# When weights are summed, split and released in a two-layer decoder trunk on one core

## The chip, the core and the metric

One core of one Trainium2 chip. The metric is the device time of one execution in microseconds (us); the kernel before has been run three times, and its median is the time that counts. Traces are of one profiled execution. Engines: PE (TensorE), DVE (VectorE), ACT (ScalarE), POOL (GpSimd) and SP (SyncE, which here only issues DMAs).

## The reference

512 tokens of width 1024 pass through two layers. Each layer is an attention and an MLP, each followed by a scaled residual sum and a layer norm:

```python
for l in range(DEPTH):                       # DEPTH = 2
    if l < n_a: y = _mla(x, ...)             # layer A: latent attention, 8 heads
    else:       y = _swa(x, w_q, sinks, w_o, k_band, v_band, rel_bias)  # layer B
    x = _layernorm(alpha * x + y, ln_mix_g[l], ln_mix_b[l])
    x = _layernorm(alpha * x + _mlp(x, mlp_w_up[l], mlp_w_down[l]), ...)
```

`_mlp` is `h = relu(x @ w_up); (h * h) @ w_down` with an inner width of 4096. `_swa` is attention in a sliding window of 128 tokens: 16 query heads of 64 on 4 key and value heads, a bias per head and distance, and a learned sink in the softmax's denominator. Everything is fp32.

## The kernel before

**Products.** PE multiplies in a shorter format (fp32r), so each operand is split into a high and a low part (`split`): ACT copies the high part (L77), DVE or POOL subtracts it from the original to give the low part (L81), and each product is made of three matmuls (L105). So every weight tile costs a DMA into a raw tile, an ACT copy `wh<-raw` of about 1.06 us, and a subtraction `wl<-raw,wh` before PE can use it.

**The stream of weights.** All weights stand in one list, `stream`, in the order of their use. `weights(name)` takes the next one for PE and, ahead of that, prepares others (`prep`: DMA, copy, subtraction are put into the program there): up to AHEAD = 4 tiles ahead on a ring of four `wh` and four `wl` tiles and two raw tiles, but never past `state["hold"]`. `prepare(n)` raises the hold by n and prepares up to it. Where in the program `prep` is called decides, with priorities and the times that a scheduler assigns, where the copy and the subtraction stand in the queues of ACT, DVE and POOL. Queues are served in order: an instruction that waits holds up all behind it. `behind(x)` adds an order after x; `pin` fixes a place.

**The MLP** multiplies in seven products instead of eight (as in Strassen's scheme); some of their weights are sums of two tiles. `grown` (L190 to L201) splits the tile as it is and then lets a DMA from POOL's queue add the next tile to it in place (L200, `accum_op=ALU.add`). The first weights of an MLP are made aside of the ring (`aside`) while the attention's output is still being projected. Two of them are grown: their accumulate DMAs are issued at 165.8 us in layer A and at 648.7 us in layer B.

**Layer norm** of a block t of 128 tokens (`layer_norm`, L428 to L443): DVE aggregates mean and variance (L434), POOL raises the variance to -1/2 (`rsqrt_of`, L413: the inverse deviation `rs`), DVE subtracts the mean and multiplies by the gain (L437), then multiplies by `rs` and adds the offset (L440). In the MLP's input the block is then turned by PE (`XFactors.turn`, L678: eight transposes into two banks) and copied by ACT and DVE (L682, L683, L689). Blocks go 0 to 3; POOL's queue holds the accumulate DMAs ahead of `rs` of block 0.

**The start of layer B** (`begin`, L589 to L618): keys of the first tokens, then two turnings of token blocks (`turn_tokens`, L452, split at L361 and L81) with values between them. The value weights `w_v` are released by `state["hold"] = len(stream)` at L598.

**Attention of layer B** (545 to 631 us) runs through `run_steps` (L533): for each head u it issues the scores of head u+2, some filling work (`fill`: queries of later heads, two heads to a weight tile of `w_sq`, and from head 11 on the output projection), the turning of head u and the mix of head u-1. Per head:
- PE makes scores; DVE adds the bias and takes the maximum (L1332, L1336); ACT takes exponentials (L1340) and the sink's (L1344, into `ri`); DVE adds and inverts (L1345, L1346); POOL multiplies (L1347, L1349).
- `turn`: PE transposes the probabilities into two banks, four transposes for the first half (128x512) and three for the second (128x384), L1360 and L1362. ACT copies each half (`pth`, L77) and DVE subtracts (`ptl`, L81). The first half's copy is ordered behind the latest exponential in the program. A later turning can use the bank when `ptl` is done.
- `mix`: PE multiplies by the values; ACT copies a half (`low`, L1391), DVE adds (L1392). After an odd head ACT copies `oh` (L77) and POOL subtracts `ol`.
- `queries`: eight groups of three matmuls; ACT and DVE put the two heads' queries aside (L1303, L1304). The bias tile comes by a DMA (L1283).

The weights inside this loop are prepared by `weights("w_sq")`, at the start of each tile's use.

Of the kernel before, what the change touches and what calls it, by code (L numbers as in the profile page):

```python
# [11 lines left out]
ALU = mybir.AluOpType  # L12
# [13 lines left out]
SQH, SKVH, SHD = 16, 4, 64  # L26
# [15 lines left out]
AHEAD_S, AHEAD_B = 3, 2  # L42
# [6 lines left out]
def build(tc, nc, io, out):  # L49
    with ExitStack() as top:  # L50
# [11 lines left out]
        def nm(s):  # L62
            n_names[0] += 1
            return f"{s}_{n_names[0]}"
# [21 lines left out]
        def pe(ins):  # L86
            tc.keep_in_program_order(ins)
# [3 lines left out]
        def behind(pair):  # L91

            both = ExitStack()
            for ins in pair or ():
                both.enter_context(tc.issue_after(ins.ins))
            return both

        def pin(ins):

            if pinned[0]:  # L100
                pe(ins)
# [8 lines left out]
            return [(sh, mh), (sh, ml), (sl, mh)]  # L110


        stream, off_ring = [], []

        fetchers, at_hand, fetched = {}, {}, set()

        def tiles_of_weights(aside=None):

            if aside:
                return aside()  # L120
            wh = wp.tile([P, 1024], F32R, tag="wh", bufs=4, name=nm("wh"))
            wl = wp.tile([P, 1024], F32R, tag="wl", bufs=4, name=nm("wl"))
            return wh, wl

        def raw_tile():
            return wp.tile([P, 1024], F32, tag="raw", bufs=2, name=nm("raw"))
# [40 lines left out]
        def queue_seven(name, key, chunk):  # L167

            quads = {}

            def half(a, jp):
                if a not in quads:
                    if (key, a) == ("U", "a"):
                        quads[a] = xp.tile([P, 4, 512], F32, tag="xt", bufs=8, name=nm("wq"))
                    elif (key, a) == ("U", "b"):
                        quads[a] = gp.tile([P, 4, 512], F32, tag="gb", bufs=1, name=nm("wq"))
                    else:
                        quads[a] = mlp_pool[0].tile([P, 4, 512], F32, tag="quad" + a, bufs=1, name=nm("wq"))  # L180
                return quads[a][:, 2 * jp : 2 * jp + 2, :]

            def flat(ap):
                return ap.rearrange("p a b -> p (a b)")

            def grown(a, jp, *more, aside=None):
                wh, wl = tiles_of_weights(aside)
                after = None
                if aside:
                    after = state.pop("plain", None)  # L190
                elif (key, a, jp, bool(more)) == ("U", "b", 0, True):
                    after = state.get("s4")
                elif (key, a, more) == ("U", "a", (1, 0)):
                    after = state.pop(("s2", jp), None)
                with behind(after):
                    state["last"] = split(
                        wh, wl, flat(half(a, jp)), keep=(a, bool(more)) == ("b", True) and key == "U"
                    )
                if more:
                    nc.gpsimd.dma_start(half(a, jp), chunk(*more, jp), accum_op=ALU.add)  # L200
                return wh, wl  # L201

            def loaded(a, jp, at, *more, aside=None):
                pe(nc.sync.dma_start(half(a, jp), chunk(*at, jp)))
                return grown(a, jp, *more, aside=aside)

            def alone(jp, aside=None):
                raw = raw_tile()
                pe(nc.sync.dma_start(raw.rearrange("p (a b) -> p a b", a=2), chunk(1, 0, jp)))
                wh, wl = tiles_of_weights(aside)  # L210
                with behind(state.pop("f1", None) if key == "D" else None):
                    split(wh, wl, raw)
                return wh, wl

            of = {
                1: lambda jp, aside=None: loaded("a", jp, (0, 0), 0, 1, aside=aside),
                5: lambda jp: grown("a", jp, 1, 1),
                6: lambda jp: grown("a", jp, 1, 0),
                4: lambda jp: grown("a", jp),
                2: alone,  # L220
                3: lambda jp: loaded("b", jp, (1, 1), 0, 1),
                7: lambda jp: grown("b", jp),
            }

            def add(n, asides=(None, None)):
                for jp, aside in enumerate(asides):
                    make = (lambda jp=jp, aside=aside: of[n](jp, aside)) if aside else (lambda jp=jp: of[n](jp))
                    stream.append((name, make))
                    off_ring.append(aside is not None)

            return add
# [52 lines left out]
        first_v = len(stream)  # L284
# [9 lines left out]
        state = {"next": 0, "at": 0, "hold": 0}  # L294
# [6 lines left out]
        def prepare(n):  # L301

            state["hold"] += n
            while state["next"] < state["hold"]:
                prep(state["next"])
                state["next"] += 1
# [20 lines left out]
        class Feat:  # L327
# [11 lines left out]
            def turn(self, t):  # L339
                turn_tokens(t, self)  # L340
# [65 lines left out]
        half = cp.tile([P, 1], F32, name="half")  # L406
# [3 lines left out]

        def rsqrt_of(v):
            r = sp.tile([P, 1], F32, tag="rs", bufs=8, name=nm("rs"))
            nc.gpsimd.tensor_tensor(r, v, half, ALU.pow)  # L413
            return r


# [13 lines left out]
        def layer_norm(t, gb, dst):  # L430

            x = xs[t]
            mv = sp.tile([P, 2], F32, tag="mv", bufs=4, name=nm("mv"))
            pin(nc.vector.bn_aggr(mv, stats[t]))  # L434
            stats[t] = None
            r = rsqrt_of(mv[:, 1:2])
            pin(nc.vector.scalar_tensor_tensor(x, x, mv[:, 0:1], gb[0], ALU.subtract, ALU.mult))  # L437
            cuts = (0, 512, 768, D) if dst is None and t == NT - 1 else (0, D)
            for c in map(slice, cuts, cuts[1:]):
                state["norm"] = nc.vector.scalar_tensor_tensor(x[:, c], x[:, c], r, gb[1][:, c], ALU.mult, ALU.add)  # L440
                pin(state["norm"])
                if dst is None:
                    nc.sync.dma_start(out[t * P : (t + 1) * P, c], x[:, c])  # L443
# [86 lines left out]
                    for t in range(NT):  # L530
                        self.evac(t, slice(512, D), bs[t])

        def run_steps(units, ahead, scores, turn, mix, fill, per, lag, rest):  # L533

            total = sum(f[0] for f in fill)
            n, spent, at = len(units), 0.0, 0
            for u in range(-ahead, n):
                if u + ahead < n:  # L540
                    scores(*units[u + ahead])
                target = total * (u + ahead + 1) / (n + ahead)
                while at < len(fill) and (spent < target or fill[at][1] <= u) and fill[at][2] <= u:
                    fill[at][3]()
                    spent += fill[at][0]
                    at += 1
                if u < 0:
                    continue
                turn(*units[u])
                if u >= lag and (u - lag) % per == per - 1:  # L550
                    mix(units[u - lag][0])
            for f in fill[at:]:
                f[3]()
            for f in rest:
                f()
            for u in range(n, n + lag):
                if (u - lag) % per == per - 1:
                    mix(units[u - lag][0])
# [35 lines left out]
        def begin(src, names, evacs, between):  # L594

            state["hold"] = len(stream)  # L598
            ws = [weights(name) for name in names]

            def products(half_):
                late = []
                for w, evac in zip(ws, evacs):
                    cols = slice(half_ * 256, half_ * 256 + 256)
                    b = bank(256)
                    feat_major(src, w, b, cols)
                    late.append((evac, cols, b))
                return late

            late = products(0)  # L610
            for i, f in enumerate(between):
                with tc.high_priority():
                    src.turn(NT - 2 + i)
                late += f()

            with behind(src.last):
                for evac, *at in late:
                    evac(*at)  # L618
            for evac, *at in products(1):
                evac(*at)  # L620
# [276 lines left out]
        with tc.tile_pool(name="mla", bufs=1) as mp:  # L897
# [301 lines left out]
            fill = []  # L1199
# [32 lines left out]
        with tc.tile_pool(name="swa", bufs=1) as mp:  # L1232
# [164 lines left out]
            fill = []  # L1397
# [12 lines left out]
            for m in range(2):  # L1410
                for part in range(2):
                    queries(m, part)
            run_steps([(h, 0) for h in range(SQH)], AHEAD_B, scores, turn, mix, fill, 1, 1, [])

        gb = lambda: load_gb("mix", 1)
        with tc.tile_pool(name="mlp1", bufs=1) as mp:
# [114 lines left out]
```

## Time and profile before

| what | value |
|---|---|
| median of three runs | 996.81 us (996.02 to 997.32) |
| profiled execution | 997.58 us |
| its span in the trace | 995.8 us |
| PE busy | 983.9 us |
| DVE, ACT, POOL busy | 772.3, 555.2, 215.4 us |
| DMA moved | 149.55 MB, 150 GB/s on average |

PE is busy nearly throughout, so what counts is where PE waits, for whom, and how long. In a row of the timeline the columns are the start in us from the start of the span, the duration, the engine, the line of the kernel, the operation, the output and inputs by name, the shapes, how often, and in brackets the engine's idle time before it and what ended that. In the view of waits the columns are the sum in us, the number of waits and the longest one. Times of PE's successive matmuls overlap in the records, since they are pipelined; gaps of PE are best read from start to start.

### The profile page before, as it was taken

Reading aid. Unit: us, or ns where it says so; the run is one execution under the profiler, and the core shown is the slowest. Engines: PE = TensorE matmul, PEld = TensorE weight load, DVE = VectorE, ACT = ScalarE, POOL = GpSimd, SP = SyncE. Lnnn points to the kernel's source line nnn. Section 1 sums busy time; section 2 is a strip of 40 time slices with the busy share of each in tenths; the row PEclk is TensorE's granted clock in tenths of the full one; section 3 lists DMA queues with packets and bytes.
Section 4 is the critical chain, followed back from the end, with each engine's and each line's share of the span. In section 5 each row is a group of like instructions: output and inputs, shape, how many; then the busy total and the mean of one; then the engine's idle time right before and its main releaser. Section 6 shows DMA issues by size and latency. Waiting matters only on the chain.

```text
span 995.8 us, 15827 instructions
## 1 busy us (share of the span) xinstructions
PE 983.9 (99%) x6103; PEld 887.2 (89%) x6103; DVE 772.3 (78%) x1242; ACT 555.2 (56%) x850; POOL 215.4 (22%) x203
## 2 busy tenths in 40 slices
PE   9999999999999999999999999999999999999997
PEld 9888887998999999998898998889998999999986
DVE  6589858999768769786686778698985886898756
ACT  5556644467547547646145798546763663664620
POOL 1231001121212212210002775112131122023000
PEclk9999999999999999999999999999999999999999
DMA  7421228389789978964132212359698698798422
GB/s 261 144 88 44 70 99 241 93 180 235 141 181 241 170 170 218 225 108 148 64 106 96 85 65 75 105 149 211 179 204 186 165 217 173 166 264 143 119 90 85
DMA packets 60679, 149.55 MB, mean 150 GB/s; under 512 B 5260, under 2 KB 10301, under 8 KB 60605
## 3 DMA queue, kind: packets, MB, share of 16 engines
q0 software_dynamic: 24320, 58.73, 33.0%
q1 hardware_dynamic: 36140, 89.56, 26.7%
q8 instruction: 48, 0.79, 0.3%
q10 hardware_dynamic: 144, 0.26, 0.1%
q14 instruction: 27, 0.21, 0.1%
HBM read 146.41 MB, written 4.22 MB: 151 GB/s over the span
## 4 chain that ended last, share of the span: by engine, by line
PE 93%; DVE 2%; DMA 2%; issue 1%; ACT 1%; POOL 0%; DVEq 0%; SPq 0%; POOLq 0%; ACTq 0%
PE mm L105 85%; PE tr L105 5%; PE tr L1171 1%; DMA wq<-in_up 1%; PE tr L678 1%; PE tr L1360 1%; DMA raw<-in_w_v 1%; ACT wh L77 1%; DVE wl L81 0%; PE tr L1362 0%; DVE x L440 0%; DMA xraw<-in_xT 0%; DVE mm L1332 0%; DVE x L437 0%; POOL wq L200 0%
## 5 line engine op out<-in xcount | busy, mean ns | idle before, releaser
L105 PE MATMUL mm<-wh,fac 128*128 128x512 f32 (+1 forms) x944 | 292.6, 386 | 0.0
L77 ACT ACTIVATE wh<-wq 128x1024 fp32r<-128x1024 f32 x164 | 173.7, 1060 | 183.7 <-PE mm L105 128.3
L81 DVE TENSOR_TENSOR wl<-wq,wh 128x1024 fp32r<-128x1024 f32 x164 | 199.6, 1221 | 70.3 <-ACT wh L77 69.4
L105 PE MATMUL mm<-xth,wh 128*128 128x256 f32 (+1 forms) x928 | 243.4, 290 | 0.0
L105 PE MATMUL mm<-xth,wl 128*128 128x256 f32 (+1 forms) x800 | 233.2, 292 | 0.0
L105 PEld LDWEIGHTS mm<-wh,fac 128*128 128x128 f32 x944 | 176.2, 188 | 35.4 <-DVE fac L81 0.6
L105 PE MATMUL mm<-xtl,wh 128*128 128x256 f32 (+1 forms) x672 | 197.1, 293 | 0.0
L105 PE MATMUL mm<-wl,fac 128*128 128x512 f32 (+1 forms) x472 | 182.3, 386 | 0.0
L105 PEld LDWEIGHTS mm<-xth,wh 128*128 128x128 f32 x928 | 168.6, 192 | 3.1
L105 PEld LDWEIGHTS mm<-xth,wl 128*128 128x128 f32 x800 | 153.2, 192 | 2.6
L77 ACT ACTIVATE wh<-raw 128x1024 fp32r<-128x1024 f32 (+3 forms) x86 | 85.1, 990 | 97.6 <-PE mm L105 57.3
L200 POOL DMA_DIRECT2D wq<-in_up x64 | 77.5, 1228 | 259.4 <-DVE wl L81 191.9
L105 PEld LDWEIGHTS mm<-xtl,wh 128*128 128x128 f32 x672 | 128.7, 192 | 3.0
L81 DVE TENSOR_TENSOR wl<-raw,wh 128x1024 fp32r<-128x1024 f32 (+2 forms) x66 | 77.1, 1174 | 36.1 <-ACT wh L77 35.8
L105 PEld LDWEIGHTS mm<-wl,fac 128*128 128x128 f32 x472 | 88.8, 188 | 16.7
L200 POOL DMA_DIRECT2D wq<-in_down x48 | 42.0, 875 | 187.3 <-DVE wl L81 181.4
L81 POOL TENSOR_TENSOR wl<-raw,wh 128x1024 fp32r<-128x1024 f32 (+2 forms) x20 | 41.2, 2062 | 88.1 <-ACT wh L77 82.1
L105 PE MATMUL mm<-wh,oh 128*128 128x512 f32 x128 | 50.9, 397 | 0.0
L105 PE MATMUL mm<-wh,ol 128*128 128x512 f32 x128 | 50.1, 391 | 0.0
L105 PE MATMUL mm<-wl,oh 128*128 128x512 f32 x128 | 50.0, 391 | 0.0
L413 POOL TENSOR_TENSOR rs<-mv,half 128x1 f32<-128x1 f32 x16 | 9.9, 620 | 168.0 <-DVE mv L434 167.9
L578 DVE TENSOR_TENSOR x<-mm,x 128x512 f32<-128x512 f32 (+1 forms) x49 | 32.9, 675 | 15.8 <-PE mm L105 15.7
(222 smaller groups left out, 1816.0 us busy)
## 6 DMA issues: line engine op xcount, KB each, us to landing
wq<-in_up POOLq DMA_DIRECT2D x64, 512.0 KB, 8.6
wq<-in_down POOLq DMA_DIRECT2D x48, 512.0 KB, 6.9
wq<-in_up SPq DMA_DIRECT2D x32, 512.0 KB, 6.6
raw<-in_down SPq DMA_DIRECT2D x28, 512.0 KB, 6.6
wq<-in_down SPq DMA_DIRECT2D x24, 512.0 KB, 5.0
raw<-in_up SPq DMA_DIRECT2D x16, 512.0 KB, 4.2
raw<-in_w_o SPq DMA_DIRECT2D x8, 512.0 KB, 5.1
raw<-in_w_sq SPq DMA_DIRECT2D x8, 512.0 KB, 3.2
```

Of the source, the lines that this page charges most:

```text
L77: high = nc.scalar.activation(dst_h, src, AF.Copy)
L81: low = (engine or nc.vector).tensor_sub(dst_l, src, f32(dst_h))
L105: pe(nc.tensor.matmul(dst, st, mv, start=first and i == 0, stop=last and i == len(pairs) - 1, **kw))
L200: nc.gpsimd.dma_start(half(a, jp), chunk(*more, jp), accum_op=ALU.add)
L413: nc.gpsimd.tensor_tensor(r, v, half, ALU.pow)
L578: nc.vector.tensor_add(xs[t][:, c], b, xs[t][:, c])
L678: pe(nc.tensor.transpose(pt[:, a, :], xs[t][:, k * P : (k + 1) * P], ident))
L1171: pe(nc.tensor.transpose(pt[:, kb * P : (kb + 1) * P], p[:, kb * P : (kb + 1) * P], ident))
L1360: pe(nc.tensor.transpose(pt[:, a, 0:P], p[:, kb, P:256], ident))
```

## The change

Three edits:

1. The accumulate DMAs of the first weight sums (those made aside) are no longer issued in `grown`. They are put into a list, `later`, and issued in `layer_norm` at block 1, ordered behind that block's inverse deviation.
2. In `begin`, the hold is raised in steps: one value weight at first, the second after the first turning, all the rest after the second turning.
3. In layer B's attention the hold is set to what has been prepared. One weight is prepared right after the turnings of heads 0, 2, 4, 6, 8 and 10, and after head 10 the hold is lifted.

```diff
-        stream, off_ring = [], []
+        stream, off_ring, later = [], [], []
...
                 if more:
-                    nc.gpsimd.dma_start(half(a, jp), chunk(*more, jp), accum_op=ALU.add)
+                    def add_more():
+                        nc.gpsimd.dma_start(half(a, jp), chunk(*more, jp), accum_op=ALU.add)
+
+                    if aside:
+                        later.append(add_more)
+                    else:
+                        add_more()
                 return wh, wl
...
         def rsqrt_of(v):
             r = sp.tile([P, 1], F32, tag="rs", bufs=8, name=nm("rs"))
-            nc.gpsimd.tensor_tensor(r, v, half, ALU.pow)
+            state["rs"] = nc.gpsimd.tensor_tensor(r, v, half, ALU.pow)
             return r
...
             r = rsqrt_of(mv[:, 1:2])
+            while t == 1 and later:
+                with behind((state["rs"],)):
+                    later.pop(0)()
             pin(nc.vector.scalar_tensor_tensor(x, x, mv[:, 0:1], gb[0], ALU.subtract, ALU.mult))
...
-        def run_steps(units, ahead, scores, turn, mix, fill, per, lag, rest):
+        def run_steps(units, ahead, scores, turn, mix, fill, per, lag, rest, turned=None):
...
                 turn(*units[u])
+                if turned:
+                    turned(u)
...
-            state["hold"] = len(stream)
+            state["hold"] = first_v + 1
             ws = [weights(name) for name in names]
...
                     src.turn(NT - 2 + i)
+                state["hold"] = first_v + 2 if i == 0 else len(stream)
                 late += f()
...
-            run_steps([(h, 0) for h in range(SQH)], AHEAD_B, scores, turn, mix, fill, 1, 1, [])
+
+            state["hold"] = state["next"]
+
+            def more_weights(u):
+                if u % 2 == 0 and u <= 10:
+                    prepare(1)
+                if u == 10:
+                    state["hold"] = len(stream)
+
+            run_steps([(h, 0) for h in range(SQH)], AHEAD_B, scores, turn, mix, fill, 1, 1, [], more_weights)
```

## The prediction

> **What bounds the kernel now.** I read the page first (span and busy time), then the waits of TensorE (PE), then the timeline around each wait that the change touches.
>
> ```profile
> span 995.8 us, 15827 instructions
> ...
> PE 983.9 (99%) x6103; PEld 887.2 (89%) x6103; DVE 772.3 (78%) x1242; ACT 555.2 (56%) x850; POOL 215.4 (22%) x203
> ```
>
> PE is busy for all but 11.9 us of the span. What no edit of order can reach, the start and the tail, is in those 11.9 too. So the change can only win what its own stages lose in waits, and it can lose as much as it makes PE wait anew. The waits of PE by releaser:
>
> ```profile
> PE tr L1360 <- DVE ptl L81: 1.7, 3, 0.9
> ...
> PE tr L678 <- DVE x L440: 0.8, 1, 0.8
> ...
> PE tr L452 <- DVE xtl L81: 0.3, 1, 0.3
> PE mm L105 <- DVE xth L361: 0.2, 1, 0.2
> ```
>
> Each of the three parts of the diff has its row here. L678 is the first turning of the MLP's input in layer A (part 1, the first weight sums). L452 and L361 stand in the turnings with the value weights (part 2). L1360 is the turning of probabilities in layer B's attention (part 3). The four rows give 3.0 us. Counted from start to start (below) the gaps are a little wider, 3.8 us in all. That is the most that the change could win: 0.4% of 996.81.
>
> **Part 1, the first sums behind the inverse deviation.** The timeline of layer A at 165 to 172 us, then of layer B at the same place, and the group of all the inverse deviations (least, median and longest ns):
>
> ```profile
> 165.80 2.59 POOL L200 DMA_DIRECT2D wq<-in_up  x2 [47.48 <-DVE w_fac L81]
> ...
> 168.28 1.32 DVE L437 SCALAR_TENSOR_TENSOR x<-x,mv,gb 128x1024 f32<-128x1024 f32 x1
> 168.33 1.66 POOL L413 TENSOR_TENSOR rs<-mv,half 128x1 f32<-128x1 f32 x1
> ...
> 170.03 1.28 DVE L440 SCALAR_TENSOR_TENSOR x<-x,rs,gb 128x1024 f32<-128x1024 f32 x1 [0.44 <-POOL rs L413]
> 170.16 0.39 PE L105 MATMUL mm<-wh,ol 128*128 128x512 f32 x1
> ...
> 171.37 0.44 PE L678 MATMUL tr<-ident,x 128*128 128x128 f32 x2 [0.82 <-DVE x L440]
> ```
>
> ```profile
> 651.16 1.32 DVE L437 SCALAR_TENSOR_TENSOR x<-x,mv,gb 128x1024 f32<-128x1024 f32 x1
> 652.58 1.28 DVE L440 SCALAR_TENSOR_TENSOR x<-x,rs,gb 128x1024 f32<-128x1024 f32 x1
> ```
>
> ```profile
> L413 POOL TENSOR_TENSOR rs<-mv,half x16: 547/550/1663, 168.3 to 989.8; 128x1 f32<-128x1 f32 x16
> ```
>
> POOL issues the two DMAs from 165.80 to 168.39, and the inverse deviation then takes 1.66 us, where the median of the 16 is 0.55. L440 waits 0.44 for it. In layer B, where L440 has not to wait, it starts 1.42 after L437 (652.58 - 651.16). With the DMAs out of the way L440 should start at 168.28 + 1.42 = 169.70 instead of 170.03: **0.33 us won**. PE's gap here is 171.37 - (170.16 + 0.23) = 0.98, with 0.23 the spacing of these matmuls; the other 0.65 stays, since L437 and L440 themselves are late on a DVE without a pause before them. In layer B there is no wait, and nothing to win. Bounds: 0 if the 1.66 comes again, 0.98 if all goes; I take 0.33, as the layer B rows show the same two instructions undisturbed.
>
> A rule speaks against this term. The Trainium skill, "SBUF — State Buffer", section "Who interferes with whom", says that a DVE instruction with two SBUF inputs and a GpSimd instruction that reads SBUF exclude each other, and the later one waits for the whole of the earlier. By it L437 (from 168.28 to 169.60) held the inverse deviation, with or without the DMAs, and the 0.33 would be 0. The median of 0.55 in the row above speaks against it as the rule for all, since layer B's L440 could not start 1.42 after L437 under it.
>
> The price is that the two sums start later. They now follow the second norm's inverse deviation:
>
> ```profile
> 172.96 0.55 POOL L413 TENSOR_TENSOR rs<-mv,half 128x1 f32<-128x1 f32 x1 [2.97 <-DVE mv L434]
> ```
> ```profile
> 656.03 0.55 POOL L413 TENSOR_TENSOR rs<-mv,half 128x1 f32<-128x1 f32 x1 [4.25 <-DVE mv L434]
> ```
> ```profile
> wq<-in_up POOLq DMA_DIRECT2D x64, 512.0 KB, 8.6
> ```
> ```profile
> 186.18 1.09 ACT L683 ACTIVATE xf<-tr 128x512 f32<-128x512 f32 x2 [3.53 <-PE tr L678]
> ```
> ```profile
> 668.84 1.09 ACT L683 ACTIVATE xf<-tr 128x512 f32<-128x512 f32 x2 [3.53 <-PE tr L678]
> ```
>
> Issues at 173.51 and about 174.8 (half of 2.59 each); 8.6 us to landing gives 183.4. ACT's copy of the landed weight (1.06, a row below) then ends at 184.5, ahead of L683, which is queued behind it, at 186.18. In layer B the same sum is 656.58 + 1.3 + 8.6 + 1.06 = 667.5 against 668.84. No wait, with 1.7 and 1.3 us to spare: **cost 0**. These 3.53 us of ACT's idle time are the cover; a landing of 10 us in layer B would use it up, and each us beyond it would delay the third turning. POOL's next work there is the third inverse deviation, far behind both issues.
>
> **Part 2, the value weights.** In the order of instructions that the changed program gives each engine, both value weights' copies and subtractions still stand ahead of the turning's copies on ACT and DVE, exactly as before. The two waits (0.3 and 0.2) stay: **0**. This part does not do what its words say.
>
> **Part 3, layer B's query weights between the turnings.** PE's own order is unchanged. On ACT and DVE the weight copies move from the front of each pair of heads to behind a turning. First how the stage runs now, at heads 9 to 12 (the turnings start at 599.52, 604.91, 609.98 and, after 614.41, the second bank at 615.66):
>
> ```profile
> 599.52 0.27 PE L1360 MATMUL tr<-ident,p 128*128 128x128 f32 x1
> ...
> 600.17 0.27 PE L1360 MATMUL tr<-ident,p 128*128 128x128 f32 x1
> ```
> ```profile
> 603.20 0.60 ACT L1391 ACTIVATE low<-mm 64x512 f32<-64x512 f32 x1
> ...
> 604.88 1.06 ACT L77 ACTIVATE wh<-raw 128x1024 fp32r<-128x1024 f32 x1 [1.08 <-PE mm L105]
> 604.91 0.27 PE L1360 MATMUL tr<-ident,p 128*128 128x128 f32 x1
> ...
> 605.96 0.59 ACT L1303 ACTIVATE q<-mm 64x512 fp32r<-64x512 f32 x1
> 605.97 1.23 DVE L81 TENSOR_TENSOR wl<-raw,wh 128x1024 fp32r<-128x1024 f32 x1 [0.62 <-ACT wh L77]
> ...
> 608.71 0.39 PE L105 MATMUL mm<-wh,ol 128*128 128x512 f32 x1
> 608.74 0.43 DVE L1332 CUSTOM_DVE_ANT_0 mm<-mm,bias 128x256 f32<-128x256 f32 x1
> ...
> 609.18 0.66 DVE L81 TENSOR_TENSOR ptl<-tr,pth 128x512 fp32r<-128x512 f32 x1
> ...
> 609.98 0.30 PE L1360 MATMUL tr<-ident,p 128*128 128x128 f32 x1 [0.89 <-DVE ptl L81]
> ...
> 610.79 0.30 PE L1360 MATMUL tr<-ident,p 128*128 128x128 f32 x1 [0.18 <-DVE ptl L81]
> ...
> 611.04 0.27 PE L1360 MATMUL tr<-ident,p 128*128 128x128 f32 x1
> ...
> 611.41 0.49 ACT L77 ACTIVATE pth<-tr 128x384 fp32r<-128x384 f32 x1 [0.88 <-PE tr L1360]
> ...
> 611.80 0.62 ACT L77 ACTIVATE oh<-o 128x512 fp32r<-128x512 f32 x1
> ...
> 612.32 0.36 ACT L1340 ACTIVATE p<-mm,nb 128x128 f32<-128x128 f32 x1
> ...
> 614.01 0.31 ACT L1344 ACTIVATE ri<-nb,sink 128x4 f32<-128x4 f32 x1
> ...
> 614.20 0.61 ACT L77 ACTIVATE pth<-tr 128x512 fp32r<-128x512 f32 x1
> ```
> ```profile
> 615.66 0.33 PE L1360 MATMUL tr<-ident,p 128*128 128x128 f32 x1 [0.65 <-DVE ptl L81]
> ```
>
> The eleventh head's turning could have started at 608.71 + 0.23 = 608.94 and starts at 609.98: 1.04 lost. Its second bank loses 610.79 - 610.45 = 0.34, the next head's second bank 615.66 - 614.84 = 0.82 (four transposes of 0.11 after 614.41). Together **2.2 us**: all that part 3 can win.
>
> A bank is free again when DVE has subtracted its half (ptl). In the changed order of ACT, heads 5, 7 and 9 do what today only head 11 does (611.41 to 614.20): they copy the second half first, then the output's high part (oh), and the first half only behind the next exponentials, with the previous head's low part between. Count from a turning's start: last transpose 0.65 (600.17 - 599.52), to ACT's copy 0.37 (611.41 - 611.04), to oh 0.39, to the next 0.52, low 0.60, exponentials to ri 1.69 (614.01 - 612.32), to the first half's copy 0.19, copy 0.61, subtraction 0.66, to PE 0.14 (609.98 - 609.84): 5.82. PE needs the bank one head (604.91 - 599.52 = 5.39) and four transposes (0.43) later: 5.82. It is a draw. I take 0.1 us for each of three heads, **0.3 lost**; bounds 0 and 0.82 each, the price of head 11's second bank.
>
> Head 10 is worse. Its last weight's copy and subtraction (wh, then wl on DVE, needed only at the end of the stage) now stand directly ahead of the copies of head 10 that release the bank for head 11. From turning 9: 4.41 up to the first half's copy (as above), copy 0.61, the fifth weight's copy 1.06, exponentials 1.69, q 0.59, ri 0.19, the sixth weight's copy 1.06, on DVE wl 1.23, scores 0.43, ptl 0.66, to PE 0.14: 12.07. Successors start about 0.1 ahead of a recorded end where nothing waits (614.20 against 614.01 + 0.31), so I take 11.9. Today it is 609.98 - 599.52 = 10.46, so turning 11 starts 1.44 later. Part comes back: the two subtractions of head 10 then stand back to back, which frees the second bank in time (0.3 of the 0.34), and the 0.82 becomes about 0.74. Net 1.44 - 0.30 - 0.08 = **1.06 lost**. Bounds: -2.2 if no wait is left, +1.6 by the full durations.
>
> **Sum.** -0.33 + 0 + 0 + 0.3 + 1.06 = +1.0 us. The profiled execution took 997.58 us (span 995.8 and 1.8 around it), 0.77 above the median of the runs shown; the difference is put on the median: 996.81 + 1.0 = **997.8 us**.
>
> **The rivals.**
> 1. Slower: heads 5, 7 and 9 each pay head 11's 0.82 at the next head's second bank. For: they take over its order, and the loop is a draw. Against: behind head 11 PE comes back after 4.43 us (614.41 - 609.98, no queries left), behind these heads after 5.39. It decides where the loop passes 5.82; at 6.64 the price is 3 x 0.82 = 2.5 in place of 0.3: 996.81 - 0.33 + 1.06 + 2.5 = 1000.0.
> 2. Faster: no wait is left at heads 10 to 12. For: today ACT idles 1.08 ahead of the weight's copy and DVE 0.62 ahead of its subtraction; a weight that comes later finds its buffer free and costs no idle time. Against: in head 10 the same copy and subtraction stand ahead of what frees the bank. It decides if ptl of head 10 is done 9.3 us after turning 9, 2.5 ahead of my sum: 996.81 - 0.33 - 2.2 = 994.3.
> 3. No effect of part 1: L437, begun 0.05 ahead (168.28 against 168.33), holds the inverse deviation to its own end, DMAs or not, so the 1.66 comes again. For: 168.33 + 1.66 ends 0.39 after L437. Against: the median of 0.55. Its price is the 0.33: 996.81 + 0.3 + 1.06 = 998.2. It is the rule of "SBUF — State Buffer" in the Trainium skill, above, that would do this.
> That part 2 changes nothing is in the forecast already.
>
> **Chances.** A measurement of this kernel can tell about 0.2% (2.0 us) from no change. Forecast 0.58, rival 1 0.17, rival 2 0.13, rival 3 0.12. Faster by over 0.2%: rival 2 but for a sliver, 0.12. Slower: rival 1 and a twentieth of the forecast, whose bounds end at -0.33 + 1.6 + 0.5, 0.22. The same: 0.66. The range takes in rival 1 with 0.3 above it and leaves out rival 2: 995.2 to 1000.3.
>
> **What would show it.** Layer A: L413 at about 168.3 with 0.55, L440 at 169.7, the first turning (L678) some 0.3 sooner after the last matmul. The two sums issued from 173.5, and ACT's copy ended before L683. Waits of L452 and L361 as today. Turning 11 some 11.9 after turning 9, waiting 2.4 for ptl; turnings 6, 8 and 10 with a second bank that waits 0.1 or less. The forecast is wrong if the ptl waits of L1360 add up to under 1 us (rival 2) or to over 5 (rival 1), or if ACT waits for a sum's landing past 186 or 668 and a third turning comes late.

## The result, and the profile after

The changed kernel takes 1000.18 us (median of 6 runs, 999.60 to 1000.67), against 996.90 us for the kernel before (6 runs): ratio 1.0033, 95% interval 1.0020 to 1.0046. So it is slower by 3.3 us, with an interval of 2.0 to 4.6. The prediction's range held the time by 0.12 us, but its likeliest case, no measurable change, did not come.

The profiled execution of the changed kernel took 999.60 us, with a span of 997.8. It is the fastest of the six, while that of the kernel before (997.58) is slower than all six of its runs, so the two traces differ by only 2.0 us where the medians differ by 3.3. First PE's waits in it, in the columns of the prediction (us in total, times, longest):

```profile
PE tr L1372 <- DVE ptl L81: 3.6, 3, 2.5
PE mm L105 <- POOL zeros L350: 1.0, 1, 1.0
PE mm L105 <- DVE ql L81: 0.5, 2, 0.2
PE mm L105 <- DVE a L808: 0.2, 1, 0.2
```

Lines have moved by 12 in the attention: L1372 is the old L1360. The waits of the turnings for `ptl` have grown from 1.7 to 3.6. The waits of L678 and L452 are gone, which looks like a success of parts 1 and 2; the runs below say what that is worth.

PE has the same 6103 instructions in the same order in both traces, so one can subtract the starts of the same matmul. Four places stand out beside the start of the kernel. At 171 us the changed kernel gets back 1.03 us, at 517 us 0.65 us, at 220 us it loses 0.46 us, and in layer B's attention it loses 2.45 us. The attention alone can be read from one row of each trace: all the transposes of a kernel's first kind, with the starts of the first and the last (least, median and longest ns of one stand ahead of them). Kernel before, then after:

```profile
L1360 PE MATMUL tr<-ident,p x64: 270/272/328, 551.9 to 630.2; 128*128 128x128 f32 x64
```
```profile
L1372 PE MATMUL tr<-ident,p x64: 270/272/329, 551.5 to 632.3; 128*128 128x128 f32 x64
```

From the first head's turning to the last one's it is 78.3 us before and 80.8 after: 2.5 lost. Where, the timeline of the changed kernel tells, by the gaps from start to start against those of before: head 5's turning comes 0.63 late, the second banks of heads 6, 8 and 10 come 0.13, 0.18 and 0.18 late, and head 11's turning comes 1.61 later than before, of which 0.39 comes back at the next two banks. PE there:

```profile
578.15 0.30 PE L1372 MATMUL tr<-ident,p 128*128 128x128 f32 x1 [0.48 <-DVE ptl L81]
...
612.39 0.30 PE L1372 MATMUL tr<-ident,p 128*128 128x128 f32 x1 [2.50 <-DVE ptl L81]
```

And ahead of head 11, ACT and DVE of the changed kernel:

```profile
608.47 1.08 ACT L77 ACTIVATE wh<-raw 128x1024 fp32r<-128x1024 f32 x1
609.42 0.98 ACT L77 ACTIVATE pth<-tr 128x512 fp32r<-128x512 f32 x2
```
```profile
608.06 0.30 DVE L1344 CUSTOM_DVE_ANT_0 mm<-mm,bias 128x128 f32<-128x128 f32 x1 [2.04 <-PE mm L105]
...
610.10 1.19 DVE L81 TENSOR_TENSOR wl<-raw,wh 128x1024 fp32r<-128x1024 f32 x1
611.21 0.42 DVE L1344 CUSTOM_DVE_ANT_0 mm<-mm,bias 128x256 f32<-128x256 f32 x1
...
611.56 1.15 DVE L81 TENSOR_TENSOR ptl<-tr,pth 128x512 fp32r<-128x512 f32 x2
```

That is the order of the prediction: the sixth weight's copy (608.47) ahead of head 10's copies (609.42), its subtraction (610.10) and a score ahead of `ptl` (611.56), and 2.5 us of waiting for it. But DVE's own queue ends last in it, and not ACT's copies: DVE waits 2.04 for PE's scores of head 13, works from 608.06 on without a pause in the view, and takes up the weight at 610.10, when ACT's copy of it has been done since 609.55 (608.47 + 1.08). Head 5 has another cause, which the prediction did not have:

```profile
573.38 2.38 POOL L81 TENSOR_TENSOR wl<-raw,wh 128x1024 fp32r<-128x1024 f32 x1
```
```profile
575.07 0.71 DVE L1357 TENSOR_TENSOR sm<-sm,ri 128x4 f32<-128x4 f32 x1 [0.28 <-ACT ri L1356]
575.71 0.42 DVE L1344 CUSTOM_DVE_ANT_0 mm<-mm,bias 128x256 f32<-128x256 f32 x1
```

The sum of head 6 (128x4 elements, 0.16 us as a rule) takes 0.71 us, and it ends at 575.78, when POOL's subtraction of a weight ends (573.38 + 2.38 = 575.76). DVE's subtraction that frees head 5's bank is queued behind it.

### The profile page after: what moved, and what is told of

Its sections match the earlier page's. It is cut to its first block, busy times and chain, and to the rows that moved or that the text cites. A ratio compares the mean times of both kernels' runs of the same rounds, so it can differ in the third digit from the quotient of the medians.

```text
span 997.8 us, 15805 instructions
## 1 busy us (share of the span) xinstructions
PE 985.1 (99%) x6103; PEld 888.0 (89%) x6103; DVE 773.3 (77%) x1242; ACT 554.1 (56%) x850; POOL 215.1 (22%) x203
## 4 chain that ended last, share of the span: by engine, by line
PE 87%; DVE 4%; DMA 3%; ACT 3%; issue 2%; POOL 0%; DVEq 0%; SPq 0%; ACTq 0%; POOLq 0%
PE mm L105 80%; PE tr L105 4%; DMA wq<-in_up 2%; ACT wh L77 1%; ACT p L1352 1%; PE tr L1183 1%; PE tr L1372 1%; DMA raw<-in_w_sq 1%; DVE mm L1344 1%; DVE x L449 0%; DMA raw<-in_w_qr 0%; DVE wl L81 0%; DVE x L446 0%; DMA raw<-in_w_h 0%; PE tr L690 0%
```

## The experiments

Theory T: the time is lost in the attention (part 3), in three places: head 5 behind a DVE sum that POOL holds up, the second banks of heads 6, 8 and 10, and head 11 behind the sixth weight. Parts 1 and 2 do not move the median. Rival R: the later accumulate DMAs of part 1 push later traffic back (the 0.46 us at 220 us), and the attention is the smaller part.

Each experiment is compared in five rounds with the kernel before on the same chip; its number is the ratio with the 95% interval. The changed kernel's row is the result above. The last column is the attention's length, read from the row of transposes as above, less the 78.3 of before; such a row is good to about 0.1.

| run | what it is | ratio (95% interval) | attention, us |
|---|---|---|---|
| changed kernel | all three parts | 1.0033 (1.0020 to 1.0046) | +2.5 |
| e1_part1 | part 1 alone | 1.0002 (0.9993 to 1.0011) | 0.0 |
| f1_part2 | part 2 alone | 0.9996 (0.9987 to 1.0005) | 0.0 |
| e2_part3 | part 3 alone | 1.0024 (1.0015 to 1.0032) | +2.5 |
| e3_late6 | sixth weight behind head 10 | 1.0028 (1.0018 to 1.0039) | +3.1 |
| e4_m7_dve | one subtraction from POOL to DVE | 1.0020 (1.0011 to 1.0029) | +1.8 |
| f3_so3_m7 | that, and the sixth weight's low part to POOL | 1.0010 (1.0001 to 1.0019) | +1.1 |
| f2_halves | halves in order | 1.0052 (1.0039 to 1.0064) | +5.1 |
| f4_low_late | low part behind exponentials | 1.0075 (1.0062 to 1.0087) | +7.0 |
| g1_hold_before | before, sixth weight held back | 1.0049 (1.0037 to 1.0062) | +0.2 |
| g2_hold_part1 | the same with part 1 | 1.0038 (1.0025 to 1.0050) | +0.2 |
| g3_hold_after | changed kernel, sixth weight held back | 1.0053 (1.0039 to 1.0066) | +1.6 |
| h1_so3_part1 | before with part 1, sixth low part to POOL | 1.0001 (0.9992 to 1.0010) | 0.0 |

**One part alone.** Part 1:

```diff
-                    nc.gpsimd.dma_start(half(a, jp), chunk(*more, jp), accum_op=ALU.add)
+                    ...   # as in the change: into `later`, issued behind the second rs
```

> Only the first weight sums are moved; the rest is the kernel before. Theory T (the loss is made in layer B's attention, part 3; part 1 wins a little): the first turning of layer A's MLP waits 0 to 0.6 us for DVE's norm instead of 0.8, no new wait behind it, time 0.3 to 1.0 us under the kernel before (ratio 0.9990 to 0.9997). Rival R (the later accumulate DMAs push the MLP's weight traffic back; the 0.46 us gap at 220 us in the changed kernel's trace is theirs): the gap at 220 us is there again, and the time is 0.5 to 1.5 us over the kernel before.

Measured: no change (996.98 against 996.61). The turning in layer A waits 0.4 instead of 0.8, and there is no gap at 220 us. R falls as the main cause: part 1 alone costs nothing that can be measured (the interval allows 0.7 us of gain and 1.1 of loss). The gap at 220 us, which R leaned on, is in 3 of the 10 traces with part 1 (0.46, 0.18, 0.14) and in none of the 4 without; whether part 1 makes it likelier was not settled. T's gain is not seen in the time either. The traces have a sign of it: set beside the kernel before, PE gains 0.4 to 1.0 us at the turning of 171 us in all ten with part 1, against 0.1, 0.15 and 1.0 in the other three without it.

Part 2:

```diff
-            state["hold"] = len(stream)
+            state["hold"] = first_v + 1
...
+                state["hold"] = first_v + 2 if i == 0 else len(stream)
```

> Only the value weights' hold is changed. Theory T: every engine's queue holds the same instructions in the same order as in the kernel before, so part 2 does nothing: ratio 0.999 to 1.001, and the waits at 513 to 517 us are there or not by the landing of the second value weight alone. Rival: part 2 makes the second value weight land sooner (the changed kernel's trace had it 0.6 us sooner in the span): the wait at the second turning of tokens is gone and the ratio is 0.9995 or less.

Measured: no change, and each engine's queue is the same, instruction by instruction. But the wait at 517 us was gone in this trace, as it was in the changed kernel's and, without part 2, in e2_part3's; with part 2 it was there in e3_late6 (0.5). So that wait comes and goes with the landing of the second value weight. Here is its copy on ACT, before and after:

```profile
514.27 1.06 ACT L77 ACTIVATE wh<-raw 128x1024 fp32r<-128x1024 f32 x1 [3.85 <-DMA raw<-in_w_v]
```
```profile
513.66 1.06 ACT L77 ACTIVATE wh<-raw 128x1024 fp32r<-128x1024 f32 x1 [2.91 <-DMA raw<-in_w_v]
```

The DMA was issued at 508.37 and 508.61 in the two spans, so it took 5.9 and 5.1 us. One trace of each kernel had suggested a gain that is none.

Part 3:

```diff
+            state["hold"] = state["next"]
+            def more_weights(u):
+                if u % 2 == 0 and u <= 10:
+                    prepare(1)
...
```

> Only the query weights are moved between the turnings; the first sums and the value weights are as before. T: the attention's own waits of the changed kernel come back whole (0.6 at head 5, 0.1 to 0.2 at heads 6, 8 and 10, about 2.6 at head 11), 2.3 us more than before, time 999 to 1000.5 (ratio 1.002 to 1.0036). R: at most half of the measured 3.3 us, time under 998.5.

Measured: 999.26 against 996.61. All the waits of the changed kernel's attention are there again. Its row:

```profile
L1362 PE MATMUL tr<-ident,p x64: 270/272/333, 550.2 to 631.0; 128*128 128x128 f32 x64
```

80.8 us, the same as with all parts to about a tenth. Part 3 is the loss: 2.4 us by the trace (2.39 by the starts of the same matmuls) and 2.4 by the ratio.

**Head 11: the sixth weight.** It is ordered behind head 10's copies:

```diff
+                with behind(state["turned"] if u == 10 else None):
                     prepare(1)
```

> The changed kernel, but the sixth weight's copy and subtraction are ordered behind those of head 10's turning. T: head 11's turning no longer waits (under 0.3 instead of about 2.5), which shows that this weight is what it waited for; the two weight copies now stand ahead of head 11's own copies on ACT, so 1.5 to 3 us of the loss come back at the second bank of head 12; time 998.5 to 1000.5. A rival in which head 11 waits for the exponentials or for the probabilities and not for the weight keeps a wait of over 2 us at head 11.

Measured: 999.90 us, and head 11's turning no longer waits at all. PE's waits of this run in the attention:

```profile
PE mm L105 <- DVE o L1404: 2.1, 1, 2.1
PE tr L1372 <- DVE ptl L81: 1.8, 2, 1.5
```

The edit moved more than the weight, though: of head 13's four scores, which stand ahead of `ptl` on DVE in the changed kernel, three now come behind it. So this run alone does not show how much of the 2.5 was the weight's; two runs below do (f3_so3_m7, g3_hold_after). The loss only moved: 1.5 at the second bank of head 12, as T had it, and 2.1 more that T did not have, since the fifth weight's copy went behind head 10 as well and both held up `low` and with it the bank of a mix. The stretch got 0.6 us longer, not shorter.

**Head 5: who holds DVE.** The last query weight's low part is subtracted by DVE:

```diff
-            queue("w_sq", io["w_sq"][m], nc.gpsimd if m > 1 else nc.vector)
+            queue("w_sq", io["w_sq"][m], nc.gpsimd if 1 < m < 7 else nc.vector)
```

> The changed kernel, but the low part of the last query weight is subtracted by DVE instead of POOL, in a stretch where DVE idles 1.7 us. T: in the changed kernel POOL's subtraction (2.38 us) held up DVE's small sum of head 4 (0.71 instead of 0.16 us, ending with POOL's instruction), and the turning of head 5 came 0.6 us late; with POOL free, that sum takes 0.16 to 0.25 us, head 5's turning waits under 0.2, and the time is 0.4 to 0.7 us under the changed kernel. Rival: the 0.71 is no lock but a late input; then the wait at head 5 stays at 0.5 or more.

(The sum is that of head 6, made while head 4 is turned; the expectation calls it head 4's.) DVE of this run at that place:

```profile
574.52 0.17 DVE L1357 TENSOR_TENSOR sm<-sm,ri 128x4 f32<-128x4 f32 x1
574.60 0.43 DVE L1344 CUSTOM_DVE_ANT_0 mm<-mm,bias 128x256 f32<-128x256 f32 x1
```

With POOL free the sum takes 0.17, head 5's turning does not wait, and the attention is 0.66 shorter than with the change. So POOL's subtraction, which held up DVE's sum until its own end (the lock of the expectation), is the cause at this head. The ratios alone (1.0020 and 1.0033) could not have shown it; the traces do.

**Both, without DVE's subtraction at head 10:**

```diff
-            queue("w_so", io["w_so"][c], nc.gpsimd if c in POOL_SO else nc.vector)
+            queue("w_so", io["w_so"][c], nc.gpsimd if c in (*POOL_SO, 3) else nc.vector)
```

> The changed kernel, with the last query weight's low part on DVE and the sixth weight's low part (an output weight) on POOL instead of DVE. T: head 5 no longer waits (under 0.1); head 11 waits for ACT's copy of the sixth weight alone and no longer for DVE's subtraction of it (1.23) and the scores behind it: 1.0 to 1.6 instead of 2.5; time 997.3 to 998.6. Rival: the wait at head 11 is ACT's alone, then it stays over 2.0 and the time over 998.6.

Measured: 998.03 us.

```profile
PE tr L1372 <- DVE nb L1348: 1.4, 1, 1.4
...
PE mm L105 <- ACT p L1352: 0.7, 1, 0.7
```

Head 11 waits 1.4 instead of 2.5, so about 1.1 of its wait was DVE's part of the weight. The rest is not ACT's, as T had it:

```profile
608.30 0.98 ACT L77 ACTIVATE pth<-tr 128x512 fp32r<-128x512 f32 x2
```
```profile
606.94 0.30 DVE L1344 CUSTOM_DVE_ANT_0 mm<-mm,bias 128x128 f32<-128x128 f32 x1 [2.04 <-PE mm L105]
...
609.37 0.69 DVE L81 TENSOR_TENSOR ptl<-tr,pth 128x512 fp32r<-128x512 f32 x1
```

Both halves are copied at 609.28, and DVE, which has waited 2.04 for PE's scores and worked since 606.94 without a pause in the view, comes to `ptl` at 609.37. Time is lost again at 618 us, where a matmul of the output projection waits 0.7 for the exponentials.

**The order of the halves:**

```diff
-                            split(pth[:, 0:2, :], ptl[:, 0:2, :], pt)
+                            first = split(pth[:, 0:2, :], ptl[:, 0:2, :], pt)
...
+                        with behind(first):
                             split(flat(pth)[:, c], flat(ptl)[:, c], flat(pt)[:, 0:384])
```

> The changed kernel, but each head's second half is copied and subtracted behind the first, so that heads 5, 7, 9 and 11 no longer take the second half first. T: the length of ACT's loop is what makes PE wait, not the order of the halves; now both banks come free late, so the first bank waits too: turnings 6, 8, 10 and 12 wait 0.4 us or more each, head 11's 2.5 stays, time 1000.5 to 1002.5. Rival: the turned order itself costs the 0.1 to 0.2; then the waits at 6, 8 and 10 go, and the time is 0.3 to 1.0 under the changed kernel.

Measured: 1002.41 us. Turnings 8 and 10 are 0.5 late each and 12 is 2.0 late; turning 6 is not late, where T expected it. Taking the second half first, as the changed kernel does at odd heads, is no cost of its own: it is what keeps the first bank free in time when ACT is behind.

**The length of ACT's loop:**

```diff
+                with behind((state["exp"],)):
                     nc.scalar.activation(low, b[hi, :], AF.Copy)
```

> The changed kernel, with the copy of a mix's half (low) ordered behind the latest exponentials. T: the loop of heads 5, 7 and 9 is 0.5 to 0.6 us shorter than PE's way back to the bank, so the waits of 0.1 to 0.2 at the second banks of heads 6, 8 and 10 go; the 0.5 at head 5 and the 2.5 at head 11 stay; time 0.3 to 0.8 under the changed kernel. Rival: those waits are DVE's, not ACT's; then they stay and so does the time.

Measured: 1004.43 us, 4.3 over the changed kernel where T expected a little under. The waits at the second banks of heads 6, 8 and 10 did go, as T said. But turnings 7 and 9 came 0.80 and 0.83 late and turning 11 3.34 later than before. DVE's sums in this run, and POOL's subtractions:

```profile
586.61 0.72 DVE L1357 TENSOR_TENSOR sm<-sm,ri 128x4 f32<-128x4 f32 x1 [0.44 <-ACT ri L1356]
...
598.28 0.74 DVE L1357 TENSOR_TENSOR sm<-sm,ri 128x4 f32<-128x4 f32 x1 [0.45 <-ACT ri L1356]
```
```profile
584.91 2.40 POOL L81 TENSOR_TENSOR wl<-raw,wh 128x1024 fp32r<-128x1024 f32 x1
...
596.59 2.41 POOL L81 TENSOR_TENSOR wl<-raw,wh 128x1024 fp32r<-128x1024 f32 x1
```

584.91 + 2.40 = 587.31, and the sum ends at 587.33; 596.59 + 2.41 = 599.00, and it ends at 599.02. The small shift put DVE's sum of each even head into POOL's subtraction, the hold-up of head 5 at every pair. How much of the 0.8 at each turning is this hold-up and how much the later `low` was not separated.

**Holding the sixth weight back.** Three kernels: the kernel before, the same with part 1, and the changed kernel.

```diff
+            state["hold"] = [n for n, _ in stream].index("w_so") + 3
             run_steps(...)
```

> The kernel before, with one thing changed: the weight that the changed kernel makes sixth (the fourth output weight, used only at the end of the stage) is held back until the heads are through. Theory T: what made head 11 wait 1.0 us even before is this weight's copy and subtraction in the pair of heads 10 and 11; without it the turning of head 11 waits under 0.3 and its second bank under 0.2, the second bank of head 12 0.4 to 0.8 as before; time 0.6 to 1.8 under the kernel before (ratio 0.9982 to 0.9994). Rival: the weight is missed at the end of the stage, where PE then waits for it, and the time is the same or more.

> As the run before, with part 1 (the later weight sums) as well: a version that might beat both. T: the same waits in the attention, and 0 to 0.5 us less in layer A, where part 1 lets the second step of the norm start 0.34 sooner but PE waits for it only in some executions; ratio 0.9978 to 0.9994.

In the changed kernel the hold is simply not lifted at head 10:

```diff
-                if u == 10:
-                    state["hold"] = len(stream)
```

> The changed kernel, with only the sixth weight held back until the heads are through. T: of the 2.5 us at head 11 at most 0.7 is left (the fifth weight's copy still stands in ACT's chain), the second bank of head 12 waits 0.9 or less, the 0.5 at head 5 and the 0.1 to 0.2 at heads 6, 8 and 10 stay; time 997.5 to 999.0. Rival: the fifth weight or the exponentials alone hold head 11, and over 1.5 us of its wait stay.

Measured: 1001.79, 1000.89 and 1001.95, all three slower, by the mechanism of the first expectation's rival: between 634 and 656 us they lose 4.5, 4.5 and 3.8 us. In the first of them head 11's turning came 0.54 sooner than in the kernel before, where T had 0.7 or more, its second bank another 0.35, and the second bank of head 12 1.03 later. Then the weight is missed at the end of the stage:

```profile
648.56 0.50 PE L105 MATMUL mm<-wh,oh 128*128 128x512 f32 x1 [0.91 <-ACT wh L77]
...
649.82 0.50 PE L105 MATMUL mm<-wl,oh 128*128 128x512 f32 x1 [0.76 <-DVE wl L81]
```
```profile
647.45 1.06 ACT L77 ACTIVATE wh<-raw 128x1024 fp32r<-128x1024 f32 x1 [3.00 <-DMA raw<-in_w_so]
```

Its raw tile is free only when it is copied, so the last output weight's DMA behind it is late as well (ACT's last copy waits 3.0 us for it), and PE loses 4.3 us between 620 and 654 us. In the changed kernel (third run) head 11 waited 1.0 instead of 2.5: with the sixth weight gone, part of the wait stays, more than the 0.7 of the expectation. From start to start the turning is then only 0.08 later than in the kernel before, so the sixth weight is all but this of the 1.61 that the change added there.

**A version that might beat both**, the kernel before with part 1 and with the sixth low part on POOL:

> The kernel before with part 1 and with the sixth weight's low part subtracted by POOL (idle there for 3.8 us) instead of DVE; the weight is made in its old place. T, from the run that did the same to the changed kernel: head 11's turning waits 0.5 to 0.8 instead of 1.0, its second bank 0.1 instead of 0.3, the second bank of head 12 nothing instead of 0.8, but the scores of head 14 come 0.9 later; with 0 to 0.5 from layer A the time is 0.3 to 1.3 us under the kernel before (ratio 0.9987 to 0.9997), which the interval may not tell from no change. Rival: POOL's subtraction holds the probabilities up or blocks DVE, and the time is the same or more.

Measured: 996.68 against 996.48, no change. The second bank of head 12 lost 0.71 of its wait, and 0.87 was lost again, as expected (not at the scores of head 14, but at a matmul of the output projection behind the scores of head 15); head 11's turning did not come sooner. No version here beat the kernel before.

## Why the prediction was partly right

**Part 1: right in its mechanism, and of no weight.** The step was "0.33 us won" at L440. With part 1 the second step of the norm starts 1.41 after the first (168.16 and 169.57 in the changed kernel), without it 1.75 (168.28 and 170.03 before, 167.16 and 168.91 in e2_part3): 0.34. What PE makes of that depends on when DVE's weights have landed. In e2_part3, which does not have part 1, DVE came there 1.1 us sooner and PE did not wait at all. The landing of the later sums was covered, as reckoned: in layer B ACT waited for the second one until 668.65 in the changed kernel, and the copies of the third turning began at 670.88, when PE had made them ready.

**Rival 3 was right about the cause and wrong about the effect.** The first inverse deviation of a norm with part 1, then that of part 3 alone:

```profile
168.20 0.55 POOL L419 TENSOR_TENSOR rs<-mv,half 128x1 f32<-128x1 f32 x1 [48.96 <-DVE mv L440]
```
```profile
167.21 1.66 POOL L413 TENSOR_TENSOR rs<-mv,half 128x1 f32<-128x1 f32 x1
```

The 1.66 comes again to the hundredth without part 1, and POOL's instruction ends 0.39 after DVE's L437 (167.16 + 1.32 = 168.48; 167.21 + 1.66 = 168.87). The Trainium skill, "SBUF — State Buffer", section "Who interferes with whom", says that the two exclude each other and that the order in which they are issued decides. The traces agree in part: POOL's instruction is held up in some cases, but most that start behind DVE's by the trace are not; the last section has the numbers. In the four traces without part 1 the one of layer A's first block is always long, in the ten with part 1 never. So that part 1 moves the long one away from there is shown, and rival 3's claim that the DMAs make no difference does not hold.

**Part 2: right.** Its term was 0, and the run gives 0.9996 (0.9987 to 1.0005).

**Part 3: the sum was short, 1.36 where the trace has 2.45.** By its terms:

| term | predicted | in the traces |
|---|---|---|
| second banks behind heads 5, 7, 9 | 0.3 | 0.49 |
| heads 10 to 12 | 1.44 - 0.30 - 0.08 = 1.06 | 1.61 - 0.34 - 0.05 = 1.22 |
| head 5's turning | 0 | 0.63 |

Head 10 came close: turning 11 starts 12.27 after turning 9 (600.12 and 612.39) where the prediction had 11.9, and waits 2.50 where it had 2.4. (By that count it is 1.81 later than before, not 1.44; this holds head 10's second bank, which the 0.3 of the prediction counts a second time.) That the sixth weight does it is shown by f3_so3_m7 and g3_hold_after. The way there was another, though: the prediction added up ACT's copies to DVE's subtraction, and in the trace DVE comes to it only at 610.10, from its scores, when ACT has been done for 0.55. That the two ways take nearly the same time is luck. The step that failed is the one that took DVE's subtractions for a bank to follow ACT's copies without delay at every head but the eleventh. It left out that POOL's subtraction of a weight, moved to another place in the pair of heads, can hold DVE. The trace of before had a sign of it, in the group of these sums (least, median, longest ns) and the one long one:

```profile
L1345 DVE TENSOR_TENSOR sm<-sm,ri x16: 157/162/1627, 543.5 to 623.4; 128x4 f32<-128x4 f32 x16
```

An instruction on 128x4 elements with a median of 0.16 and a longest of 1.63 us looks held up: it ran beside a POOL subtraction (from 549.27 for 2.41), and both ended at 551.7. That wait cost PE nothing there, so no view of waits showed it.

**Rival 1 had the right number, 1000.0, for a wrong reason.** Its mechanism was 0.82 at each of three second banks. They cost 0.13 to 0.18 each. What stood in for it was head 5 and the rest of the table. Without this rival the range would not have reached the measured time (the bounds of the forecast end at 1.77 us, under the 2.0 that it calls slower), so that the range held it is luck too. The measured 3.3 us (2.0 to 4.6) hold both the trace's 2.45 and the 2.4 of part 3 alone; whether the three parts together cost more than part 3 alone was not settled.

## What to carry to other kernels

When an edit moves an instruction to another place in an engine's queue, price it in two ways: what is queued behind it on its own engine, and what runs beside it on another engine, since the two can hold each other up (here POOL's subtraction and DVE's small sum). A group of small instructions whose longest is ten times its median showed this here before any wait did. And gaps that depend on when a DMA lands differ from execution to execution by more than an edit of this size is worth, so a gain at such a gap needs runs of the part alone.

## What the runs showed of the hardware

**Whether DVE holds POOL up changes with a hundredth of a microsecond.** In all fourteen traces I set each inverse deviation of POOL beside the DVE instruction of its block that subtracts the mean (L437 in the kernel before). Of 224, 31 started ahead of DVE's. In 137 cases POOL's started 0.042 to 0.045 us after DVE's, and it took 0.55 to 0.56 every time. In 56 cases it started 0.055 to 0.057 after it, and in 15 of these it took 1.65 to 1.66 and ended 0.40 to 0.43 after DVE's. What decides among these 56 stays open. With part 1 the long one can come back at another block: in e1_part1 it is that of the third block, the first one behind the moved DMAs, and there PE does not wait for it.

```profile
181.19 1.65 POOL L419 TENSOR_TENSOR rs<-mv,half 128x1 f32<-128x1 f32 x1 [5.45 <-DVE mv L440]
```

**PE's clock fell during a long wait.** In f4_low_late head 11 waited 4.23 us, up to 615.30. The granted clock (the column behind PE's busy time and its instructions) was halved for the next 5 us:

```profile
612.00:615.30 3.30, 0.00 (x1) 0.75 0.42 150
615.30:617.00 1.70, 1.70 (x8) 0.50 0.78 289
617.00:619.00 2.00, 2.00 (x12) 0.50 0.01 4
619.00:621.00 2.00, 2.00 (x10) 0.63 0.00 0
621.00:624.00 3.00, 3.00 (x24) 1.00 0.02 5
```

That is some 2 us of this run's 7. If the clock is full or half, as in these rows, the 0.75 in the first of them is 1.65 us at half (0.25 x 3.30 / 0.5): it fell about 2.6 us into the wait, which began at 611.07. The 2.5 us at head 11 of the changed kernel left the clock at 1.00. The Trainium skill, "TensorE: Matmul & The Clock Gate", section "Part 1: The HAM clock gate (the "warmup" mystery)", puts the bound at an idle window of about 3.4 us. Of these two waits only the one that is longer than that lowered the clock, but the clock fell before 3.4 us of the wait had passed. The held-back kernels do not fit so simply. In the first of them the clock fell to 0.61 and 0.53 from 650 to 654 us, behind two waits of 0.91 and 0.76 us:

```profile
648.50:650.00 1.50, 0.68 (x2) 1.00 1.01 376
650.00:652.00 2.00, 2.00 (x6) 0.61 1.05 407
652.00:654.00 2.00, 2.00 (x6) 0.53 0.88 277
```

In the second (g2_hold_part1) the same matmuls wait 0.96 and 0.76, and the clock stays at 1.00:

```profile
648.23 0.50 PE L105 MATMUL mm<-wh,oh 128*128 128x512 f32 x1 [0.96 <-ACT wh L77]
649.49 0.50 PE L105 MATMUL mm<-wl,oh 128*128 128x512 f32 x1 [0.76 <-DVE wl L81]
```
```profile
649.50:651.50 2.00, 2.00 (x9) 1.00 1.04 420
651.50:653.50 2.00, 2.00 (x11) 1.00 0.94 338
```

So such waits alone do not decide it, and what else does stays open.
